# Two-block transformer forward on one Trainium2 core: convolution taps held in program sequence, and unsplit float32 products of attention weights and values in block 2

## The chip, the core and the metric

The kernel runs on one core of one Trainium2 chip. The core has a matrix engine (TensorE, PE in the profile, its weight loads PEld), a vector engine (VectorE, DVE), an activation engine (ScalarE, ACT), a general engine (GpSimd, POOL) and a queue that issues transfers (SyncE, SP). The metric is device time of one execution in microseconds, the median of several. TensorE runs at one of two levels of its clock, 1.2 or 2.4 GHz; the profile gives the granted share (0.50 or 1.00).

## What is computed

Two different transformer blocks of two layers each, on 256 tokens of width 1024, in float32.

Block 1 has a second stream of 256 context tokens. Each of its layers runs a token mixer with three branches, a gated merge of them, and a SwiGLU feed-forward. The first layer runs both streams (512 columns), the second only the first one (256). Two pieces of the mixer matter here:

```python
def conformer_conv(h, w_glu, conv_w, conv_b, ln_g, ln_b, w_proj):
    u = h @ w_glu
    u = u[..., :CONV_CH] * jax.nn.sigmoid(u[..., CONV_CH:])
    u = depthwise_conv(u, conv_w, conv_b)        # width 31, 512 channels
    u = layer_norm(u, ln_g, ln_b)
    return jax.nn.silu(u) @ w_proj

def diff_attend(q, k, v, lam):                   # 8 heads, two halves of 64 each
    s = jnp.einsum('bhiqd,bhikd->bhiqk', q, k).astype(jnp.float32) * (HEAD_DIM ** -0.5)
    p = jax.nn.softmax(s, axis=-1)
    a = (p[:, :, 0] - lam * p[:, :, 1]).astype(v.dtype)
    return jnp.einsum('bhqk,bhkd->bhqd', a, v)
```

Block 2 has a layer with causal attention under a top-k mask (12 heads), a layer with three dilated groups (4 heads each, one softmax over the three), and in both an attention over 256 memory tokens (4 heads). Heads are 64 wide. Each is a softmax over scores and then the product of its weights p with the values v, `einsum('bhsm,bmhd->bshd', p, v)`. A feed-forward follows in each layer, and one norm at the end.

## The kernel before

Activations lie transposed, channels on the 128 partitions and tokens along the free axis. Nearly all products are made in three passes: each operand is split in a rounded part (hi, in the type fp32r that TensorE takes in one pass) and the rest (lo), and `mm3` (lines 160 to 166) issues hi by hi, hi by lo and lo by hi into one PSUM tile. Weights come by DMA as `raw` tiles of 1 MB. ACT writes their hi (`whi`, line 154) and DVE, for a few of them POOL, subtracts it from raw (`wlo`, line 155). PSUM has eight banks: six tiles `p` for linear layers and scores, two tiles `tr` for transposes, sums and products with values.

The program is a list of steps. `merge` interleaves side steps with the main ones in proportion to a cost. `emit` runs the steps in that order and so records the instructions. A scheduler then orders them on each engine by its own model of time and readiness, which may put an instruction far ahead of where it was recorded. `pin` (line 454) takes one instruction out of that freedom: it stays in the sequence of the program. Before the change only memsets and some transfers are pinned.

**The convolution** (`conv_tap`, lines 783 to 798). For channel tiles m = 0 and 1 a tap is one DVE instruction, acc = u * w + acc (line 796; the first one, with the bias, line 790). For m = 2 and 3 ACT multiplies (line 793) and POOL adds (line 794). There are 31 taps for each tile and layer. The first 20 steps go beside the projections of head pair 0, the rest in four equal parts beside the four rounds of `qkv(pr+1)` and `att(pr)`: the projections of the next pair of heads and the attention of this one.

**The round around it.** `qkv` makes q and k tiles in PSUM, and DVE and ACT take them out: a shuffle (718), two multiplies and an add of the rotary embedding (719, 720, 726), the split (257 and 258), and the split of the context half (260 and 261). The last of them, line 261 for k or for a scaled q, releases the `p` tile. `att_s` makes scores (`scores2`, line 743: two halves of 64 partitions, one instruction each in turn), DVE takes the maximum (853), ACT the exponential (856), DVE the reciprocal, a factor and the difference (860, 862, 863). `att_t` transposes the result (PE, 871), ACT copies it out (873), and `att_v` multiplies it with the values in unsplit float32 (881).

**Block 2's products with values.** `val_split` (1239) splits the values, `at_split` (1265) transposes a tile of softmax weights (PE, 1270) and splits it with ACT and DVE (257 and 258), and `values` (1250) makes for each of two heads three passes with 128 columns of values, of which only the head's own 64 rows of the result are used. Head 0 goes to columns 0 to 255 of a `tr` tile and head 1 to columns 256 to 511. Two ACT (1261) and two DVE instructions (1263) on 64 partitions each write the split output `O`, which the output projection multiplies. There are 12 calls of `values`: six in the top-k layer, two in the dilated one, and two for the memory in each.

Of the kernel before, what the change touches and what calls it, by code (L numbers as in the profile page):

```python
# [7 lines left out]
F32R = mybir.dt.float32r  # L8
I32 = mybir.dt.int32
AF = mybir.ActivationFunctionType  # L10
ALU = mybir.AluOpType
# [19 lines left out]
class Piece:  # L31
    hi = lo = prep = at = None
# [13 lines left out]
class Kern:  # L46
# [701 lines left out]
    def mixer1(self, l, hs, N, evac_y, mid):  # L748

        nc, a = self.nc, self.a  # L750
# [3 lines left out]
        V = {}  # L754
        P = lambda name: self.par[name, l]
# [27 lines left out]
        def conv_tap(m, k):  # L783
            if k == 0:
                V["ca", m] = self.slot()
            acc = V["ca", m][:, :N].rearrange("p (s t) -> p s t", s=nseg)
            u = V["u", m][:, :nseg, k + 1:k + 257]
            w = self.convw[l][:, 4 * k + m:4 * k + m + 1]
            if k == 0:
                nc.vector.tensor_scalar(acc, u, w, P("conv_b")[:, m:m + 1], op0=ALU.mult, op1=ALU.add)  # L790
            elif m >= 2:
                t = self.slot()[:, :N].rearrange("p (s t) -> p s t", s=nseg)
                nc.scalar.activation(t, u, AF.Copy, scale=w)  # L793
                nc.gpsimd.tensor_tensor(acc, acc, t, op=ALU.add)  # L794
            else:
                nc.vector.scalar_tensor_tensor(acc, u, w, acc, op0=ALU.mult, op1=ALU.add)  # L796
            if k == 30:
                V.pop(("u", m))

# [238 lines left out]
        out = []  # L1038
# [197 lines left out]
            nc.scalar.activation(p, p, AF.Copy, scale=r)  # L1236
        return p

    def val_split(self, ps, nh, sc=None):

        n = 64 * nh
        if n <= 256:
            t = self.slot(F32R)
            out = [t[:, :n], t[:, 256:256 + n]]
        else:
            out = [self.slot(F32R)[:, :n] for _ in range(2)]
        self.split(out[0], out[1], ps[:, :n], sc)
        return out

    def values(self, O, terms):  # L1250


        nc = self.nc
        ps = self.tr_ps()
        for h in range(2):
            for j, (v, p, c) in enumerate(terms[h]):
                self.mm3(ps[:, 256 * h + c:256 * h + 256], v, p, j == 0, j == len(terms[h]) - 1)
        hi, lo = O
        rows = [(slice(64 * h, 64 * h + 64), ps[64 * h:64 * h + 64, 256 * h:256 * h + 256]) for h in range(2)]
        for r, x in rows:  # L1260
            nc.scalar.activation(hi[r], x, AF.Copy)
        for r, x in rows:
            nc.vector.tensor_tensor(lo[r], x, hi[r], op=ALU.subtract)

    def at_split(self, p, nk, key, t, V):

        nc = self.nc
        ps = self.tr_ps()
        for k in range(nk):
            nc.tensor.transpose(ps[:, 128 * k:128 * k + 128], p[:, 128 * k:128 * k + 128], self.ident)  # L1270
        hi, lo = V[key]
        self.split(hi[:, t, :nk], lo[:, t, :nk], ps[:, :128 * nk].rearrange("p (k q) -> p k q", q=128))

    def mem_kv(self, l):

        nc, a, V = self.nc, self.a, self.v
        st = []
        Wm = a[f"l{l}_w_mem_kv_2"]

        def k_evac(m, ps):  # L1280
            if m == 0:
                V["mk", l] = self.acts(2, 256)
            self.split(*V["mk", l][m], ps[:, :256])

        self.lin(st, Wm, 0, 256, lambda: V["mh", l], 256, k_evac)

        def v_evac(t, ps):
            V["mv", l, t] = self.val_split(ps, 4)
# [87 lines left out]
    def mem_att(self, l, base, O):  # L1376

        nc, V = self.nc, self.v
        st = []

        def s_(h, t):
            if h % 2 == 0:
                V["ms"] = [self.s_ps()[:, :256] for _ in range(2)]
                self.scores2(V["qm", h // 2], V["mk", l][h // 2], slice(128 * t, 128 * t + 128), slice(0, 256), V["ms"])
            s = V["ms"][h % 2]
            V["mp", h, t] = self.softmax(s[:, :256], 256, V["rc"][:, t:t + 1])

        def n_(h, t):
            V["mp", h, t] = self.norm(*V["mp", h, t])

        def t_(h, t):
            if t == 0:
                V["mat", h] = [self.slot(F32R).rearrange("p (t k q) -> p t k q", t=2, k=2) for _ in range(2)]
            self.at_split(V.pop(("mp", h, t)), 2, ("mat", h), t, V)

        def v_(g):
            self.values(O()[base + g], [[([v[:, 128 * g:128 * g + 128] for v in V["mv", l, k]],
                                          [p[:, :, k] for p in V["mat", 2 * g + h]], 0)
                                         for k in range(2)] for h in range(2)])

        return self.pipe([(2 * g + h, t) for g in range(2) for t in range(2) for h in range(2)], s_, n_, t_, v_)
# [47 lines left out]
    def dsa(self, l):  # L1449
        nc, a, V = self.nc, self.a, self.v  # L1450
# [95 lines left out]
            V["qm", m] = p  # L1546

        def v_evac(t, ps):
            V["v", t] = self.val_split(ps, 4, V["rc"][:, t:t + 1])
# [29 lines left out]

        def t_(m, half, t):  # L1580
            if t == 0:
                V["aat", m, half] = [self.slot(F32R).rearrange("p (t k q) -> p t k q", t=2, k=2) for _ in range(2)]
            self.at_split(V.pop(("ap", m, half, t)), t + 1, ("aat", m, half), t, V)
# [12 lines left out]
    def dilated(self, l):  # L1596
# [18 lines left out]

        def v_evac(g):
            def f(t, ps):
                V["v", g, t] = self.val_split(ps, 4, V["rc"][:, t:t + 1])
            return f

        def qm_evac(m, ps):
# [61 lines left out]
        def t_(h, t):  # L1683
            if t == 0:
                for g in range(3):
                    V["aat", h, g] = [self.slot(F32R).rearrange("p (t k q) -> p t k q", t=2, k=2) for _ in range(2)]
            p = V.pop(("ap", h, t))
            for g in range(3):
                self.at_split(p[g // 2][:, 256 * (g % 2):], t + 1, ("aat", h, g), t, V)

        def v_(m):
            self.values(V["O"][m], [[([v[:, 128 * m:128 * m + 128] for v in V["v", g, k]],
                                      [p[:, k:, k] for p in V["aat", 2 * m + h, g]], 128 * k)
                                     for k in range(2) for g in range(3)] for h in range(2)])

        att = self.pipe([(2 * m + h, t) for m in range(2) for t in range(2) for h in range(2)], s_, n_, t_, v_)
# [228 lines left out]
```

## Time and profile before

| | |
|---|---|
| median of 3 runs | 2344.86 us (2341.8 to 2348.15) |
| the profiled execution, its own time | 2343.53 us |
| its span, first to last instruction | 2341.8 us |
| mean granted TensorE clock | 0.966 |
| PE busy | 2188.9 us, 93% of the span |
| DVE busy | 1642.7 us, 70% |
| ACT busy | 1090.0 us, 47% |
| POOL busy | 536.1 us, 23% |

The profiled execution took 1.7 us more than its span, and stands 1.3 us under the median. PE is busy nearly all the time, so what counts is where it is not, and where its clock is at the lower level. Line 796, the taps on DVE, holds 2% of the chain that ended last.

### The profile page before, as it was taken

Reading aid. Unit: us, or ns where it says so; the run is one execution under the profiler, and the core shown is the slowest. Engines: PE = TensorE matmul, PEld = TensorE weight load, DVE = VectorE, ACT = ScalarE, POOL = GpSimd, SP = SyncE. Lnnn points to the kernel's source line nnn. Section 1 sums busy time; section 2 is a strip of 40 time slices with the busy share of each in tenths; the row PEclk is TensorE's granted clock in tenths of the full one; section 3 lists DMA queues with packets and bytes.
Section 4 is the critical chain, followed back from the end, with each engine's and each line's share of the span. In section 5 each row is a group of like instructions: output and inputs, shape, how many; then the busy total and the mean of one; then the engine's idle time right before and its main releaser. Section 6 shows DMA issues by size and latency. Waiting matters only on the chain.

```text
span 2341.8 us, 37618 instructions
## 1 busy us (share of the span) xinstructions
PE 2188.9 (93%) x14576; PEld 1990.2 (85%) x14576; DVE 1642.7 (70%) x3315; ACT 1090.0 (47%) x2110; POOL 536.1 (23%) x545
## 2 busy tenths in 40 slices
PE   4978899999989999998999999899989999999998
PEld 3767777788888888888898999899967999998998
DVE  5585865958778855567977877765686765687665
ACT  5335565333332222233566655554456554565543
POOL 2344343221340111042333312100353000210000
PEclk9989999999999999997999999999988999999999
DMA  7311121345514555553322454465441555542553
GB/s 272 93 55 56 53 73 56 105 151 168 174 37 155 166 180 175 162 165 127 126 73 81 149 171 163 144 203 178 153 110 39 166 186 178 187 145 91 181 184 123
DMA packets 296627, 319.20 MB, mean 136 GB/s; under 512 B 20544, under 2 KB 264352, under 8 KB 296448
## 3 DMA queue, kind: packets, MB, share of 16 engines
q1 hardware_dynamic: 293072, 311.27, 41.3%
q0 software_dynamic: 2224, 3.43, 0.6%
q8 instruction: 114, 1.87, 0.3%
q10 hardware_dynamic: 1152, 2.10, 0.3%
q14 instruction: 65, 0.53, 0.1%
HBM read 315.72 MB, written 1.05 MB: 135 GB/s over the span
## 4 chain that ended last, share of the span: by engine, by line
PE 69%; DVE 18%; ACT 4%; issue 4%; DMA 2%; POOL 2%; ACTq 0%; DVEq 0%; POOLq 0%; SPq 0%
PE p L164 20%; PE p L165 19%; PE p L166 19%; DVE wlo L155 3%; DVE t L796 2%; DVE t L478 2%; PE p L743 2%; PE p L247 1%; PE p L249 1%; PE p L248 1%; PE tr L881 1%; ACT whi L154 1%; DMA mraw<-in_w_mod_dram 1%; DVE b L853 1%; PE tr L484 1%
## 5 line engine op out<-in xcount | busy, mean ns | idle before, releaser
L164 PE MATMUL p<-t,whi 128*128 128x256 f32 (+1 forms) x3724 | 1176.5, 320 | 18.3 <-ACT t L560 7.1
L166 PE MATMUL p<-t,wlo 128*128 128x256 f32 (+1 forms) x3724 | 1178.1, 318 | 10.4 <-DVE wlo L155 5.9
L165 PE MATMUL p<-t,whi 128*128 128x256 f32 (+1 forms) x3724 | 1181.5, 318 | 5.5 <-DVE t L261 1.7
L164 PEld LDWEIGHTS p<-t,whi 128*128 128x128 f32 x3724 | 716.8, 194 | 69.7 <-ACT t L560 8.3
L166 PEld LDWEIGHTS p<-t,wlo 128*128 128x128 f32 x3724 | 721.3, 194 | 55.6 <-DVE wlo L155 7.6
L165 PEld LDWEIGHTS p<-t,whi 128*128 128x128 f32 x3724 | 722.1, 194 | 50.2 <-DVE t L659 3.5
L154 ACT ACTIVATE whi<-raw 128x1024 fp32r<-128x1024 f32 (+4 forms) x487 | 491.5, 1020 | 536.0 <-PE p L165 335.1
L155 DVE TENSOR_TENSOR wlo<-raw,whi 128x1024 fp32r<-128x1024 f32 (+4 forms) x443 | 547.7, 1238 | 204.9 <-ACT whi L154 107.5
L155 POOL TENSOR_TENSOR wlo<-raw,whi 128x1024 fp32r<-128x1024 f32 (+2 forms) x44 | 103.9, 2362 | 525.7 <-ACT whi L154 507.0
L478 DVE SCALAR_TENSOR_TENSOR t<-mraw,big,t 128x512 f32<-128x512 f32 x224 | 173.2, 811 | 16.9 <-DMA mraw<-in_w_mod_dram 15.2
L794 POOL TENSOR_TENSOR t<-t,t 128x512 f32<-128x512 f32 (+1 forms) x120 | 131.8, 1098 | 181.0 <-ACT t L793 171.3
L299 POOL TENSOR_TENSOR t<-t,t 128x256 f32<-128x256 f32 (+1 forms) x27 | 25.3, 935 | 426.1 <-ACT t L297 375.8
L260 ACT ACTIVATE t<-t 128x256 fp32r<-128x256 f32 (+1 forms) x115 | 54.3, 473 | 146.5 <-DVE t L689 110.9
L594 POOL TENSOR_TENSOR t<-t,t 128x256 f32<-128x256 f32 (+1 forms) x68 | 69.6, 1053 | 225.3 <-ACT t L596 224.6
L743 PE MATMUL p<-t,t 64*128 64x256 f32 (+2 forms) x528 | 80.9, 380 | 30.1 <-DVE t L261 18.8
L247 PE MATMUL p<-whi,t 128*128 128x256 f32 x352 | 102.7, 292 | 0.8 <-ACT t L856 0.8
L249 PE MATMUL p<-whi,t 128*128 128x256 f32 x352 | 100.4, 285 | 0.0
L248 PE MATMUL p<-wlo,t 128*128 128x256 f32 x352 | 100.0, 284 | 0.0
L257 ACT ACTIVATE t<-p 128x256 fp32r<-128x256 f32 x76 | 29.1, 383 | 149.1 <-DVE p L726 118.3
L796 DVE SCALAR_TENSOR_TENSOR t<-u,big,t 128x512 f32<-128x512 f32 (+1 forms) x120 | 97.2, 810 | 1.8
L689 DVE TENSOR_TENSOR t<-t,p 128x256 f32<-128x256 f32 (+1 forms) x91 | 43.1, 474 | 75.6 <-PE p L166 75.5
L743 PEld LDWEIGHTS p<-t,t 64*128 64x128 f32 x528 | 52.6, 212 | 51.1 <-issue 26.3
(303 smaller groups left out, 2633.9 us busy)
## 6 DMA issues: line engine op xcount, KB each, us to landing
raw<-in_w_in_dram SPq DMA_DIRECT2D x60, 1024.0 KB, 5.1
raw<-in_l_w_gate_up_dram SPq DMA_DIRECT2D x44, 1024.0 KB, 5.1
raw<-in_w_ffn_in_dram SPq DMA_DIRECT2D x42, 1024.0 KB, 5.2
mraw<-in_w_mod_dram SPq DMA_DIRECT2D x80, 512.0 KB, 4.1
raw<-in_l_w_in_dram SPq DMA_DIRECT2D x15, 1024.0 KB, 5.1
raw<-in_l_w_down_dram SPq DMA_DIRECT2D x16, 896.0 KB, 4.9
t<-in_w_mod_dram SPq DMA_DIRECT2D x32, 256.0 KB, 5.4
raw<-in_w_attn_out_dram SPq DMA_DIRECT2D x8, 1024.0 KB, 5.3
```

The source lines that it names most:

```text
L154: nc.scalar.activation(p.hi, src, AF.Copy)
L155: eng.tensor_tensor(p.lo, src, p.hi, op=ALU.subtract)
L164: mm(ps, lh, rh, start=first, stop=False)
L165: mm(ps, lh, rl, start=False, stop=False)
L166: mm(ps, ll, rh, start=False, stop=last)
L247: mm(ps[:, :256], lh, p.hi[:, k % 4], start=k == 0, stop=False)
L248: mm(ps[:, :256], lh, p.lo[:, k % 4], start=False, stop=False)
L249: mm(ps[:, :256], ll, p.hi[:, k % 4], start=False, stop=k == 7)
L478: nc.vector.scalar_tensor_tensor(acc, w[:, k], c, acc, op0=ALU.mult, op1=ALU.add)
L743: self.nc.tensor.matmul(out[half], q[i // 2][h, qs], k[i % 2][h, ks], start=i == 0, stop=i == 2)
L794: nc.gpsimd.tensor_tensor(acc, acc, t, op=ALU.add)
L796: nc.vector.scalar_tensor_tensor(acc, u, w, acc, op0=ALU.mult, op1=ALU.add)
```

## The change

Two things. Every tap's DVE or ACT instruction is pinned (POOL's adds are not). And in block 2 neither the values nor the transposed softmax weights are split: each product with values is one float32 matmul with the head's own 64 columns, head 0 on the column half of the array that gives partitions 0 to 63 and head 1 on the other, in turn, into the same 256 columns of one `tr` tile. The output is split in one piece, by one ACT and one DVE instruction on 128 partitions.

```diff
             if k == 0:
-                nc.vector.tensor_scalar(acc, u, w, P("conv_b")[:, m:m + 1], op0=ALU.mult, op1=ALU.add)
+                i = nc.vector.tensor_scalar(acc, u, w, P("conv_b")[:, m:m + 1], op0=ALU.mult, op1=ALU.add)
             elif m >= 2:
                 t = self.slot()[:, :N].rearrange("p (s t) -> p s t", s=nseg)
-                nc.scalar.activation(t, u, AF.Copy, scale=w)
+                i = nc.scalar.activation(t, u, AF.Copy, scale=w)
                 nc.gpsimd.tensor_tensor(acc, acc, t, op=ALU.add)
             else:
-                nc.vector.scalar_tensor_tensor(acc, u, w, acc, op0=ALU.mult, op1=ALU.add)
+                i = nc.vector.scalar_tensor_tensor(acc, u, w, acc, op0=ALU.mult, op1=ALU.add)
+
+            self.pin(i)
...
-        for h in range(2):
-            for j, (v, p, c) in enumerate(terms[h]):
-                self.mm3(ps[:, 256 * h + c:256 * h + 256], v, p, j == 0, j == len(terms[h]) - 1)
-        hi, lo = O
-        rows = [(slice(64 * h, 64 * h + 64), ps[64 * h:64 * h + 64, 256 * h:256 * h + 256]) for h in range(2)]
-        for r, x in rows:
-            nc.scalar.activation(hi[r], x, AF.Copy)
-        for r, x in rows:
-            nc.vector.tensor_tensor(lo[r], x, hi[r], op=ALU.subtract)
+        n = len(terms[0])
+        for j in range(n):
+            for h in range(2):
+                v, p, c = terms[h][j]
+                nc.tensor.matmul(ps[64 * h:64 * h + 64, c:256], v, p, start=j == 0, stop=j == n - 1)
+        self.split(*O, ps[:, :256])
 
-    def at_split(self, p, nk, key, t, V):
+    def at_copy(self, p, nk, key, t, V):
...
-        hi, lo = V[key]
-        self.split(hi[:, t, :nk], lo[:, t, :nk], ps[:, :128 * nk].rearrange("p (k q) -> p k q", q=128))
+        nc.scalar.activation(V[key][:, t, :nk], ps[:, :128 * nk].rearrange("p (k q) -> p k q", q=128), AF.Copy)
...
-            self.values(V["O"][m], [[([v[:, 64 * kv:64 * kv + 128] for v in V["v", k]], [p[:, k:, k] for p in x[h]],
+            self.values(V["O"][m], [[(V["v", k][:, 64 * (kv + h):64 * (kv + h) + 64], x[h][:, k:, k],
                                       128 * k) for k in range(2)] for h in range(2)])
```

`val_copy` stands in the place of `val_split` in the same way: one ACT instruction, with the token's scale where there is one. The calls for the memory and the dilated layer change as the last one shown does.

How the instructions move on DVE in block 1's first layer, between the projections of head pair 1 and its last release of a `p` tile (line 261). `t_980<-u_766` is a tap, `wlo` a weight's lo part. Before:

```order
L796 SCALAR_TENSOR_TENSOR t_980<-u_766,big,t_980 128x512
L258 TENSOR_TENSOR t_1112<-p_1086,t_1111 128x256
L796 SCALAR_TENSOR_TENSOR t_980<-u_766,big,t_980 128x512 x9
L155 TENSOR_TENSOR wlo_1254<-raw,whi_1253 128x1024
L796 SCALAR_TENSOR_TENSOR t_980<-u_766,big,t_980 128x512
L155 TENSOR_TENSOR wlo_1258<-raw,whi_1257 128x1024
L796 SCALAR_TENSOR_TENSOR t_980<-u_766,big,t_980 128x512 x4
L718 STREAM_SHUFFLE t_1288<-p_1261 128x256
L719 TENSOR_TENSOR p_1261<-p_1261,t_610 128x256
L155 TENSOR_TENSOR wlo_1365<-raw,whi_1364 128x1024
L726 TENSOR_TENSOR p_1261<-p_1261,t_1288 128x256
```

After:

```order
L258 TENSOR_TENSOR t_1112<-p_1086,t_1111 128x256 x2
L796 SCALAR_TENSOR_TENSOR t_980<-u_766,big,t_980 128x512 x5
L155 TENSOR_TENSOR wlo_1254<-raw,whi_1253 128x1024
L155 TENSOR_TENSOR wlo_1258<-raw,whi_1257 128x1024
L718 STREAM_SHUFFLE t_1288<-p_1261 128x256
L719 TENSOR_TENSOR p_1261<-p_1261,t_610 128x256
L155 TENSOR_TENSOR wlo_1365<-raw,whi_1364 128x1024
L726 TENSOR_TENSOR p_1261<-p_1261,t_1288 128x256
L855 TENSOR_REDUCE b_1302<-p_1303 128x1
L258 TENSOR_TENSOR t_1287<-p_1261,t_1286 128x256
L855 TENSOR_REDUCE b_1302<-p_1304 128x1
L261 SCALAR_TENSOR_TENSOR t_1287<-p_1261,t_1286 128x256
```

From the start of the taps to this line 261 there are 26 taps of line 796 before, and 9 after. Before, the 60 taps of the layer stand in two runs of 30. After, those taken out of the runs stand further on, in ones and twos, between the instructions of all the rounds.

On PE, one call of `values` in the top-k layer. The tile written is its PSUM tile, the first one read holds the transposed softmax weights of one head, and the second one values. Before:

```order
L164 MATMUL tr_17633<-t_17395,t_16793 128x256
L165 MATMUL tr_17633<-t_17396,t_16793 128x256
L166 MATMUL tr_17633<-t_17395,t_16793 128x256
L164 MATMUL tr_17633<-t_17395,t_16837 128x128
L165 MATMUL tr_17633<-t_17396,t_16837 128x128
L166 MATMUL tr_17633<-t_17395,t_16837 128x128
L164 MATMUL tr_17633<-t_17407,t_16793 128x256
L165 MATMUL tr_17633<-t_17408,t_16793 128x256
L166 MATMUL tr_17633<-t_17407,t_16793 128x256
L164 MATMUL tr_17633<-t_17407,t_16837 128x128
L165 MATMUL tr_17633<-t_17408,t_16837 128x128
L166 MATMUL tr_17633<-t_17407,t_16837 128x128
```

After:

```order
L1267 MATMUL tr_17623<-big,t_17549 128x128 x2
L1259 MATMUL tr_17602<-t_17385,t_16789 64x256
L1259 MATMUL tr_17602<-t_17395,t_16789 64x256
L1259 MATMUL tr_17602<-t_17385,t_16832 64x128
L1259 MATMUL tr_17602<-t_17395,t_16832 64x128
```

Twelve matmuls of 128 output rows became four of 64, heads in turn.

## Rows read from the trace of the kernel before

**Rows 1.** The page: granted clock in 40 slices, in tenths

```profile
PEclk9989999999999999997999999999988999999999
```

**Rows 2.** Stretches: length, busy us (count) per engine, clock, DMA share, GB/s

```profile
core 0: us, PE busy (x) PEld busy (x) DVE busy (x) ACT busy (x) POOL busy (x), PEclk, DMA share, GB/s
110.00:172.00 62.00, 48.26 (x258) 41.25 (x257) 55.98 (x83) 22.77 (x47) 25.45 (x18) 0.89 0.21 68
172.00:250.00 78.00, 71.67 (x430) 59.84 (x429) 44.73 (x112) 46.79 (x119) 35.53 (x28) 0.96 0.17 55
250.00:312.00 62.00, 51.21 (x292) 42.66 (x290) 57.33 (x105) 32.66 (x85) 23.09 (x17) 0.92 0.16 52
312.00:400.00 88.00, 85.12 (x497) 70.03 (x496) 42.21 (x99) 53.80 (x130) 33.16 (x26) 1.00 0.22 73
```

**Rows 3.** Timeline of PE: start, us, instruction, count [idle before <-its end]

```profile
163.16 0.98 PE L743 MATMUL p<-t,t 64*128 64x256 f32 x3 [13.74 <-DVE t L261]
...
222.35 0.48 PE L164 MATMUL p<-t,whi 128*128 128x512 f32 x1 [2.80 <-DVE t L261]
...
281.01 0.98 PE L743 MATMUL p<-t,t 64*128 64x256 f32 x3 [5.04 <-DVE t L261]
```

**Rows 4.** Waits of PE by layer: us, times, longest

```profile
PE tr L871 <- DVE t L863: 6.9, 6, 2.5
...
PE tr L871 <- DVE t L863: 6.1, 2, 3.2
```

**Rows 5.** Timeline of DVE, taps of the first layer

```profile
141.19 11.42 DVE L796 SCALAR_TENSOR_TENSOR t<-u,big,t 128x512 f32<-128x512 f32 x9
...
153.66 0.74 DVE L796 SCALAR_TENSOR_TENSOR t<-u,big,t 128x512 f32<-128x512 f32 x1
```

**Rows 6.** Stretches, line 796 alone: DVE busy (count), clock, DMA

```profile
117.40:163.16 45.76, 29.25 (x26) 0.91 0.21 69
...
1165.50:1168.76 3.26, 1.91 (x3) 0.92 0.41 121
```

**Rows 7.** Stretches behind two of the waits, columns as in group 2

```profile
163.16:168.10 4.94, 4.94 (x13) 3.85 (x14) 4.83 (x12) 3.10 (x10) 1.77 (x2) 0.50 0.00 0
281.01:287.50 6.49, 6.49 (x17) 5.00 (x18) 4.83 (x12) 3.10 (x10) 1.70 (x2) 0.50 0.00 0
```

**Rows 8.** Timeline of PE, a call of `values` in either layer

```profile
1801.41 0.28 PE L164 MATMUL tr<-t,t 128*128 128x256 f32 x1
...
1802.74 0.41 PE L1270 MATMUL tr<-big,t 128*128 128x128 f32 x2
...
2118.84 0.39 PE L164 MATMUL tr<-t,t 128*128 128x256 f32 x1 [0.49 <-DVE t L258]
...
2123.03 0.41 PE L1270 MATMUL tr<-big,t 128*128 128x128 f32 x2
```

**Rows 9.** Timeline of PE: unsplit products (line 881), row halves (line 743)

```profile
172.43 1.06 PE L881 MATMUL tr<-t,t 128*128 128x128 f32 x8
173.42 0.38 PE L743 MATMUL p<-t,t 64*128 64x256 f32 x2
...
1740.81 0.28 PE L165 MATMUL p<-t,whi 128*128 128x256 f32 x1
1740.93 0.28 PE L166 MATMUL p<-t,wlo 128*128 128x256 f32 x1
1741.13 0.62 PE L743 MATMUL p<-t,t 64*128 64x256 f32 x6
```

**Rows 10.** Waits of PE, top-k attention, then dilated attention

```profile
PE tr L1270 <- DVE t L258: 2.8, 1, 2.8
...
PE p L164 <- ACT t L1261: 1.1, 2, 0.6
...
PE tr L1270 <- DVE t L258: 2.0, 4, 0.7
...
PE p L164 <- ACT t L1261: 1.5, 2, 0.9
```

More of the change, by code (lines that the diff above doesn't have):

```diff
@@ L1237, in norm, with val_copy @@
         return p
[L1239 to L1244, printed above, removed]
-        else:
-            out = [self.slot(F32R)[:, :n] for _ in range(2)]
-        self.split(out[0], out[1], ps[:, :n], sc)
-        return out
+    def val_copy(self, ps, nh, sc=None):
+        t = self.slot()[:, :64 * nh]
+        if sc is None:
+            self.nc.scalar.activation(t, ps[:, :64 * nh], AF.Copy)
+        else:
+            self.nc.scalar.activation(t, ps[:, :64 * nh], AF.Copy, scale=sc)
+        return t
     def values(self, O, terms):
@@ L1287, in v_evac @@
         def v_evac(t, ps):
-            V["mv", l, t] = self.val_split(ps, 4)
+            V["mv", l, t] = self.val_copy(ps, 4)
         self.lin_nat(st, Wm, 256, lambda t: [(h[:, 128 * t:128 * t + 128], lo[:, 128 * t:128 * t + 128])
@@ L1392, in t_ @@
             if t == 0:
-                V["mat", h] = [self.slot(F32R).rearrange("p (t k q) -> p t k q", t=2, k=2) for _ in range(2)]
-            self.at_split(V.pop(("mp", h, t)), 2, ("mat", h), t, V)
+                V["mat", h] = self.slot().rearrange("p (t k q) -> p t k q", t=2, k=2)
+            self.at_copy(V.pop(("mp", h, t)), 2, ("mat", h), t, V)
         def v_(g):
-            self.values(O()[base + g], [[([v[:, 128 * g:128 * g + 128] for v in V["mv", l, k]],
-                                          [p[:, :, k] for p in V["mat", 2 * g + h]], 0)
+            self.values(O()[base + g], [[(V["mv", l, k][:, 128 * g + 64 * h:128 * g + 64 * h + 64], V["mat", 2 * g + h][:, :, k], 0)
                                          for k in range(2)] for h in range(2)])
@@ L1548, in v_evac @@
         def v_evac(t, ps):
-            V["v", t] = self.val_split(ps, 4, V["rc"][:, t:t + 1])
+            V["v", t] = self.val_copy(ps, 4, V["rc"][:, t:t + 1])
         self.lin(rest, W, 1864, 256, hs, 256, qm_evac)
@@ L1581, in t_ @@
             if t == 0:
-                V["aat", m, half] = [self.slot(F32R).rearrange("p (t k q) -> p t k q", t=2, k=2) for _ in range(2)]
-            self.at_split(V.pop(("ap", m, half, t)), t + 1, ("aat", m, half), t, V)
+                V["aat", m, half] = self.slot().rearrange("p (t k q) -> p t k q", t=2, k=2)
+            self.at_copy(V.pop(("ap", m, half, t)), t + 1, ("aat", m, half), t, V)
         def v_(m):
@@ L1617, in f @@
             def f(t, ps):
-                V["v", g, t] = self.val_split(ps, 4, V["rc"][:, t:t + 1])
+                V["v", g, t] = self.val_copy(ps, 4, V["rc"][:, t:t + 1])
             return f
@@ L1685, in t_ @@
                 for g in range(3):
-                    V["aat", h, g] = [self.slot(F32R).rearrange("p (t k q) -> p t k q", t=2, k=2) for _ in range(2)]
+                    V["aat", h, g] = self.slot().rearrange("p (t k q) -> p t k q", t=2, k=2)
             p = V.pop(("ap", h, t))
             for g in range(3):
-                self.at_split(p[g // 2][:, 256 * (g % 2):], t + 1, ("aat", h, g), t, V)
+                self.at_copy(p[g // 2][:, 256 * (g % 2):], t + 1, ("aat", h, g), t, V)
         def v_(m):
-            self.values(V["O"][m], [[([v[:, 128 * m:128 * m + 128] for v in V["v", g, k]],
-                                      [p[:, k:, k] for p in V["aat", 2 * m + h, g]], 128 * k)
+            self.values(V["O"][m], [[(V["v", g, k][:, 128 * m + 64 * h:128 * m + 64 * h + 64], V["aat", 2 * m + h, g][:, k:, k], 128 * k)
                                      for k in range(2) for g in range(3)] for h in range(2)])
```

## The prediction

> **What bounds the kernel now.** I read the page first. PE is busy 93% of the span, so time can be won only where PE stands idle, works at the lower level of its clock, or does work that goes away. The page's row of the granted clock is full nearly everywhere; its slices are 58.5 us wide and hide short stretches at 0.50 [rows 1]. So I cut the stretch of the first layer's taps in four: the two in which line 796 runs in bulk (110 to 172 and 250 to 312), and the two without taps on DVE [rows 2]. The reader is to see there how DVE and PE go together. In the stretches with taps DVE is busy 55.98 and 57.33 of 62 us and PE lacks 13.7 and 10.8 us; in those without, DVE has 33 and 46 us to spare and PE lacks 6.3 and 2.9.
>
> The timeline of PE then names the three long waits [rows 3]. All end with line 261 on DVE, the release of a `p` tile at the end of a round's projections: 13.74, 2.80 and 5.04 us. The middle one is the same wait in a round without any tap ahead of it. So 2.80 is what this place costs by itself, and the rest of the other two is DVE's backlog. The timeline of DVE shows the backlog: nine taps in a row, 11.42 us, and later ones of 0.74 us [rows 5]. From the first tap to PE's restart at 163.16, 26 taps hold DVE for 29.25 of 45.76 us [rows 6].
>
> **The change, part by part**, against the profiled execution (span 2341.8, its own time 2343.53 us, which lies 1.3 us under the median of 2344.86).
>
> *Taps, first layer.* No instruction is added or removed; the 60 taps of DVE move. Ahead of the first long wait 9 taps stand instead of 26, as the order of DVE shows. The 17 that go were worth at least 17 x 0.74 = 12.6 us [rows 5] and at their mean of 29.25 / 26 = 1.12 us [rows 6] 19 us, which is more than the 10.9 us by which the wait exceeds 2.80. So I let it fall to 2.80: **-10.9**. The third wait falls likewise from 5.04: **-2.2**. PE restarts after both at the lower level: 4.94 and 6.49 us of uninterrupted work at 0.50 [rows 7], which at 1.00 would take half. I count all of the first gain and half of the second, since a wait of 2.80 us stays: -2.5 - 1.6 = **-4.1**. (With no gain in clock this term is 0; with all of it, -5.7.)
>
> Against this, taps now stand between the maximum, the factor and the difference of each attention step, and PE's transposes wait for the difference (line 871 for line 863: 6.9 us in 6 waits [rows 4], of 32 steps in this layer). The trace shows no round with taps in ones and twos. Bounds: nothing new, where every tap falls in DVE's idle time, or one tap in every step, 32 x 0.74 = 24 us, and 41 at the 1.27 us of the run of nine. I take a value near the lower bound, because DVE has 33 and 46 us to spare in the rounds that get the taps, 15 taps each: a tap in one of five steps, +5 us, less 3 us of the old 6.9 which fall in the third stretch, where the taps become fewer: **+2**.
>
> ACT's taps, pinned too, and POOL's adds behind them keep their number. ACT is busy 46.79 of 78 us in the fullest of these stretches, and POOL 35.53 [rows 2]; their idle time covers it. Without that cover ACT's split of the weights would be late, and PE with it. The queue of transfers keeps its order and moves 52 to 73 GB/s here [rows 2]: nothing.
>
> *Taps, second layer.* Two waits for line 863 make 6.1 us [rows 4], and in the 3.26 us ahead of one of them three taps hold DVE for 1.91 [rows 6]. Half of 6.1 goes, and 1.5 comes back in other steps: **-1.5** (from -6.1 to +8, the second being 16 steps with a tap of about 0.5).
>
> *Products with values, on PE.* A call before: in the top-k layer 1802.74 - 1801.41 = 1.33 us for 12 matmuls; in the dilated one 2123.03 - 2118.84 = 4.19 us for 36 [rows 8]; for the memory 12 matmuls of 256 columns at a step of 0.12 us [rows 9], 1.44. Six, two and four calls: 8.0 + 8.4 + 5.8 = 22.1 us. After: an unsplit product with 128 moving columns is two records, and four of them take 173.42 - 172.43 = 0.99 us with a change of tiling at the end [rows 9]. A change of tiling costs 0.20 instead of 0.12 us (1740.93 to 1741.13 [rows 9]), so 0.91 / 4 = 0.23 us each, and 0.46 with 256 columns. One after the other: 6 x 1.38 + 4 x 1.84 + 2 x 4.14 = 23.9 us, and the change of tiling, twice in each of 12 calls, 1.9: 25.8 in all, +3.7. In pairs, the two column halves at once: 13.9, or -8.2. The nearest row for pairs is that of the two row halves: six of 256 columns take 0.62 us [rows 9], where a step of 0.12 and a last one of 0.28 would make 0.88. So halves do run together. As each product is two records and heads alternate only by product, I add half a product a call, 12 x 0.2: **-6** (bounds -8.2 and +3.7).
>
> The Trainium skill speaks against this part. "TensorE: Matmul & The Clock Gate", Part 3, "The mechanism", says that a weight load overlaps a running matmul only if its row group differs, and column halves share their rows. By that rule the halves would not overlap so freely, and the sum would hold +3.7 in the place of -6. The trace does not bear it out for whole-array matmuls, whose weight loads lie beside other matmuls (59.84 us of loads and 71.67 of matmuls in 78 [rows 2]). No row here shows column halves. It is a rival below.
>
> *Copies around them.* `at_copy` drops 64 subtractions on DVE, and `values` halves 24 ACT and 24 DVE instructions; the 12 subtractions of the values go too. Most lie beside PE's work: nothing. On the path: PE waits four times for the subtraction to release a `tr` tile in the dilated layer, 2.0 us, which goes; the same wait of 2.8 in the top-k layer I leave, as ACT ends late there. PE waits four times for line 1261, 1.1 + 1.5 us [rows 10]; one ACT instruction instead of two takes some 0.4 off each: **-3.5** together (bounds 0 and -7.4, all four rows).
>
> Sum: -10.9 - 2.2 - 4.1 + 2 - 1.5 - 6 - 3.5 = -26.2. From 2343.5 that is 2317.3, and with the 1.3 us to the median 2318.6: **2319 us**. If the column halves were in series it would be 2328.
>
> **The rivals.**
>
> 1. *Column halves in series.* PE's order has the heads in turn, but two records of one head stand next to each other, and pairs are shown for row halves alone. Price +3.7 for -6: **2328**. Chance 0.20.
>
> 2. *DVE gives part of it back.* A tap beside a POOL add costs more (1.27 in the run of nine against 0.74 [rows 5]), and the taps go to stretches in which POOL is busy 35.53 of 78 us [rows 2]. With one tap exposed in every second step, 16 x 0.74 = 12 in the first layer for 5, and 4 for 1.5 in the second: +9.5, **2328**. Chance 0.15.
>
> 3. *The long wait is not the taps.* It could be that the `p` tile would come late anyway, since a shuffle, a weight's subtraction, maxima and splits stand ahead of its release too. Then only block 2 gains: 9.5 us or, with halves in series, nothing, **2335 to 2345**. Against it speaks the same place at 2.80 us without taps [rows 3]. Chance 0.10.
>
> 4. *Slower: the chain of each attention step takes the taps.* The 32 steps of the first layer and 16 of the second run maximum, exponential, factor, difference, transpose one behind the other. If one tap were exposed in each, it would be 32 x 1.27 = 41 for 5 and 16 x 0.6 = 10 for 1.5, +44: **2363**. It decides from 0.7 us a step on, where the new waits (33 us) eat the gain and what I had counted for them. Against it: PE has projections between a step's scores and its transposes, so that line 871 waited for line 863 8 times in 48 steps. Chance 0.05.
>
> **How the numbers follow.** The forecast holds 0.50. A measurement of this kernel tells 0.3% from no change, 7 us. Faster by more (under 2337.8): the forecast, rivals 1 and 2, and half of rival 3 would make 0.90; I take 0.05 off for rivals 1 and 2 coming together with a late restart: 0.85. Within 0.3%: 0.10. Slower: 0.05. The range goes down to 2304, where nothing new waits, line 871's 6.9 us go and the halves pair fully (about -2 - 5 - 4 - 4 against the forecast), and up to 2337, rivals 1 and 2 together.
>
> **What would show it.** Right: PE's wait at the end of round 1 under 4 us; line 796 spread over all four stretches, with DVE between 48 and 60 us in each; PE's granted clock in 110 to 172 above 0.95; a top-k call of `values` near 0.9 us; no wait of line 1270's successor for a subtraction. Wrong: PE's idle time before line 871 above 15 us in the first layer (rivals 2 and 4); a call of 1.4 us or more (rival 1); a wait above 8 us still at line 261 (rival 3).

## The result, and the profile after

The changed kernel takes 2311.3 us, the median of 4 runs (2308.62 to 2312.47); the kernel before took 2345.55 beside it (4 runs, 2341.8 to 2348.15). The ratio is 0.9847 with a 95% interval of 0.9833 to 0.9861: faster by 34 us where 26 were forecast (2319, range 2304 to 2337). The profiled span went from 2341.8 to 2308.5 us.

To see where the 33.3 us of span came from, I cut both traces at the same instructions of PE: from the last transpose of line 322 to line 316 behind the first layer's attention, from there to the second layer's attention (which ends at the transposes of line 1319, later 1315), then to block 2's top-k layer, and at both ends of its two attention parts. Each column of times is one execution, the profiled one.

| stretch | before, us | after, us | difference |
|---|---|---|---|
| first layer with its taps | 315.2 | 298.7 | -16.5 |
| from there to the second layer's attention | 726.9 | 729.3 | +2.4 |
| second layer's attention and taps | 213.4 | 212.7 | -0.7 |
| up to block 2's top-k layer | 337.0 | 336.2 | -0.8 |
| top-k attention with its memory | 147.8 | 140.4 | -7.4 |
| between | 198.7 | 198.2 | -0.5 |
| dilated attention with its memory | 111.7 | 102.4 | -9.3 |
| the rest, both ends | 291.1 | 290.7 | -0.4 |

Busy times in three of these stretches, from the view by stretches (columns as in [rows 2]), first of before, then of after:

```profile
97.10:412.30 315.20, 279.92 (x1569) 232.97 (x1569) 214.82 (x438) 163.82 (x386) 121.72 (x96) 0.95 0.19 64
...
1689.60:1837.40 147.80, 127.87 (x881) 112.90 (x880) 110.73 (x364) 84.07 (x233) 57.08 (x69) 0.87 0.32 86
...
2036.10:2147.80 111.70, 104.49 (x815) 97.46 (x815) 88.66 (x276) 66.13 (x174) 19.71 (x23) 0.94 0.33 111
```

```profile
95.90:394.60 298.70, 275.27 (x1569) 228.72 (x1569) 221.32 (x434) 165.35 (x386) 124.44 (x96) 0.97 0.20 65
...
1672.80:1813.10 140.30, 124.17 (x846) 106.89 (x847) 95.85 (x322) 78.96 (x226) 57.85 (x69) 0.84 0.33 91
...
2011.30:2113.70 102.40, 97.61 (x776) 89.23 (x776) 74.93 (x234) 64.43 (x170) 19.57 (x25) 0.93 0.38 123
```

The first layer has the same 1569 matmuls. They hold PE for 4.65 us less, since more of them ran at the upper level of the clock, and PE stands idle for 11.85 us less. In the dilated part PE's busy time falls by 6.9 us with 39 fewer matmul records, and its idle time from 7.2 to 4.8.

The same four stretches of the first layer as in [rows 2], of after:

```profile
110.00:161.00 51.00, 46.62 (x252) 39.95 (x251) 40.45 (x66) 23.16 (x45) 24.74 (x18) 0.93 0.25 83
161.00:239.00 78.00, 71.22 (x423) 58.60 (x421) 57.91 (x125) 46.55 (x116) 35.60 (x28) 0.96 0.17 55
239.00:294.00 55.00, 50.13 (x314) 42.56 (x312) 41.86 (x87) 33.70 (x86) 23.48 (x17) 0.97 0.19 58
294.00:382.00 88.00, 82.29 (x478) 67.45 (x477) 64.95 (x116) 53.23 (x127) 34.90 (x25) 1.00 0.23 73
```

These windows only come near those of before. Cut at the very instructions of PE at which [rows 2] cuts, the two stretches that held the taps become some 9 to 10 us shorter each (52.5 and 52.6 for 62), the second 0.8 us longer and the fourth some 3 us longer (91.1 for 88). In the windows shown, line 796 has 12, 17, 12 and 20 instructions in them, where it had 30, 1, 30 and none. PE's long waits, in its timeline of after, answer to [rows 3]:

```profile
152.60 0.98 PE L743 MATMUL p<-t,t 64*128 64x256 f32 x3 [4.38 <-DVE t L261]
...
209.12 0.98 PE L743 MATMUL p<-t,t 64*128 64x256 f32 x3 [2.83 <-DVE t L261]
...
266.05 0.82 PE L743 MATMUL p<-t,t 64*128 64x256 f32 x3 [2.81 <-DVE t L261]
```

13.74, 2.80 and 5.04 us became 4.38, 2.83 and 2.81. Behind the first and the third PE still restarts at the lower level, and stays there for nearly the whole of the first stretch and half of the third (0.55 and 0.74 for 0.50 and 0.50 in [rows 7]):

```profile
152.60:157.54 4.94, 4.94 (x14) 3.88 (x15) 4.86 (x11) 3.52 (x10) 2.83 (x2) 0.55 0.00 0
...
266.05:272.54 6.49, 6.49 (x24) 5.19 (x25) 6.45 (x13) 4.09 (x12) 2.82 (x2) 0.74 0.00 0
```

How long PE now waits in front of the transposes, by layer (first layer, then second; [rows 4] had 6.9 and 6.1):

```profile
PE tr L873 <- DVE t L865: 4.2, 5, 1.7
...
PE tr L873 <- DVE t L865: 8.4, 4, 2.7
```

In the first layer PE also waits more for ACT, 5.5 us in all, where before it waited 0.8 us for line 856. First the row of before, then those of after:

```profile
PE p L247 <- ACT t L856: 0.8, 1, 0.8
```

```profile
PE p L247 <- ACT t L858: 2.7, 2, 1.6
...
PE p L743 <- ACT t L875: 1.5, 2, 1.1
PE p L743 <- ACT t L891: 1.3, 1, 1.3
```

And calls of `values`, top-k, memory and dilated, in PE's timeline of after ([rows 8]); a call runs from its first matmul to the start of what follows:

```profile
1782.74 0.87 PE L1259 MATMUL tr<-t,t 128*64 128x256 f32 x8
1783.55 0.44 PE L1267 MATMUL tr<-big,t 128*128 128x128 f32 x2
...
2047.80 1.08 PE L1259 MATMUL tr<-t,t 128*64 128x256 f32 x8
2048.81 0.39 PE L164 MATMUL p<-t,whi 128*128 128x256 f32 x1
...
2091.57 2.17 PE L1259 MATMUL tr<-t,t 128*64 128x256 f32 x24
2093.67 0.44 PE L1267 MATMUL tr<-big,t 128*128 128x128 f32 x2
```

1.33 became 0.81, 1.44 became 1.01, and 4.19 became 2.10 us. Not every call runs so: the first of the top-k layer takes 1.48 us at a clock of 0.50, and the two for the memory there take 1.21 and 1.84, the second with a product of line 743 among its records. All twelve as they ran take 14.6 us, where those of before took 24.0. PE waits no more for a subtraction there: of [rows 10], 2.0 us in the dilated part are now 0.9 for ACT's copy, and the waits for line 1261 are gone.

### The profile page after: what moved, and what is told of

The parts are those of the page before. It is cut to its first block, busy times and chain, and to the rows that moved or that the text cites. A ratio compares the mean times of both kernels' runs of the same rounds, so it can differ in the third digit from the quotient of the medians.

```text
span 2308.5 us, 37343 instructions
## 1 busy us (share of the span) xinstructions
PE 2175.2 (94%) x14512; PEld 1974.4 (86%) x14512; DVE 1622.4 (70%) x3227; ACT 1085.5 (47%) x2098; POOL 535.8 (23%) x545
## 4 chain that ended last, share of the span: by engine, by line
PE 73%; DVE 15%; ACT 4%; issue 3%; POOL 2%; DMA 1%; ACTq 0%; DVEq 0%; POOLq 0%
PE p L164 21%; PE p L165 21%; PE p L166 20%; DVE wlo L155 3%; PE p L743 1%; DVE t L478 1%; DVE t L796 1%; PE tr L883 1%; PE p L247 1%; PE p L249 1%; PE p L248 1%; PE tr L484 1%; DVE b L855 1%; PE tr L1267 1%; POOL t L794 1%
## 5 line engine op out<-in xcount | busy, mean ns | idle before, releaser
L796 DVE SCALAR_TENSOR_TENSOR t<-u,big,t 128x512 f32<-128x512 f32 (+1 forms) x120 | 102.2, 851 | 0.8
```

Source lines behind the costliest of these rows:

```text
L796: i = nc.vector.scalar_tensor_tensor(acc, u, w, acc, op0=ALU.mult, op1=ALU.add)
```

## Experiments

My theory after the result: the two parts add, the taps giving what the first layer shows and block 2 what its attention shows. Times are medians; "before" stands for the runs of the kernel before on the same chip.

**Each part alone.** The first kernel has the pins and the old block 2. The second has the new block 2 and no pins; its edit against the changed kernel is shown:

```diff
-            self.pin(i)
```

> Only the taps are pinned; block 2 is as before. Theory (the two parts add, the taps are worth what the first layer shows between the traces, about 16 us): span 2326, between 2322 and 2329; the wait at line 261 at the end of round 1 falls from 13.7 to 4 to 5 us, and block 2 takes as long as before (147.8 us for the top-k part, 111.7 for the dilated part). Rival 1 (the long wait shrinks only because block 2's change moved buffers or the order elsewhere): wait above 8 us, span 2336 to 2342. Rival 2 (the taps carry more than their layer shows, since block 2 starts from other conditions): span under 2320.

Measured: 2342.84 us (10 runs), before 2344.46, ratio 0.9986 (0.9975 to 0.9997). The wait fell to 4.59 us and the first layer from 315.2 to 301.9, as expected:

```profile
152.34 0.97 PE L743 MATMUL p<-t,t 64*128 64x256 f32 x3 [4.59 <-DVE t L261]
```

Yet the kernel is hardly faster, and its span of 2340.7 us lies where rival 1 had it, for another reason. From the first layer's end to block 2's top-k layer it needs 1288.3 us where before needed 1277.3. The mean granted clock doesn't tell the two apart: over all their runs it goes from 0.962 to 0.968 here and from 0.962 to 0.966 before. Block 2's attention is not shorter, 461.0 us for 458.1 (here and below from the start of the top-k part to the end of the dilated one, with what lies between).

> Only block 2 is changed; the taps are free again. Theory (the parts add; block 2 is worth the 17 us by which its two attention parts became shorter between the traces): span 2325, between 2321 and 2328, with the first long wait back at 13 to 14 us. Rival (block 2 is worth only the 9.5 us of the prediction and the rest came with the taps): span 2331 to 2334, and the two attention parts of block 2 together shorter by about 10 us, not 17.

Measured: 2323.31 us, ratio 0.9920 (0.9903 to 0.9936). The first long wait is back at 13.70:

```profile
161.91 0.98 PE L743 MATMUL p<-t,t 64*128 64x256 f32 x3 [13.70 <-DVE t L261]
```

Block 2's attention takes 441.3 us, as in the changed kernel (440.9). So block 2 alone is worth 21 us, taps alone 1.6, and both 34: the parts don't add in these kernels. The theory holds for the stretches, and fails for the sum.

**Column halves in series.** The loops of `values` exchanged:

```diff
-        for j in range(n):
-            for h in range(2):
+        for h in range(2):
+            for j in range(n):
```

> The changed kernel with the loops of values exchanged: all products of the first head, then all of the second, on the same column halves; nothing else differs. Theory (the two column halves work at the same time when neighbours in the order use different halves): a dilated call goes from 2.1 to about 4.1 us, a top-k call from 0.8 to about 1.5, and the kernel is slower than the changed one by 8 to 12 us: span 2317 to 2321. Rival (the halves are in series anyway, or PE waits there for other engines, so that order does not matter): calls unchanged, span 2307 to 2311.

Measured: 2313.74 us, ratio 0.9869 (0.9854 to 0.9883). In its timeline of PE a top-k call and a dilated one:

```profile
1783.04 0.88 PE L1259 MATMUL tr<-t,t 128*64 128x256 f32 x8
1783.85 0.44 PE L1267 MATMUL tr<-big,t 128*128 128x128 f32 x2
...
2098.33 3.73 PE L1259 MATMUL tr<-t,t 128*64 128x256 f32 x24
2101.99 0.39 PE L166 MATMUL p<-t,wlo 128*128 128x256 f32 x1
```

The dilated call goes from 2.10 to 3.66 us: the halves do work at once, and there it takes alternation. The call with two products for each head keeps its 0.81 us, though both products of head 0 stand ahead of those of head 1. Its records start in the order of 256, 256, 256, 256, 128, 128, 128 and 128 columns, though the program has two of 256 and two of 128 of head 0 first. So PE itself brings work of the other half forward, at least two products (four records) far. With six products a head this comes too late for most of them: head 1 starts 1.57 us into the call, beside the last four of head 0's twelve records. Ten of twelve calls are of the short kind, so only the two dilated ones become longer, 3.1 us together, and the dilated part takes 104.8 us for 102.4. Both theories missed that.

The whole differs by 2.4 us, but other stretches move by more than that. Ahead of the first changed call this kernel has the changed kernel's instructions, in the same order and with the same places of its tiles, and yet the second layer's attention took 4.5 us longer (first the changed kernel, then this one):

```profile
1123.90:1336.60 212.70, 196.61 (x1462) 180.35 (x1460) 174.12 (x385) 129.04 (x288) 71.43 (x95) 1.00 0.31 101
```

```profile
1123.29:1340.53 217.24, 199.57 (x1462) 183.33 (x1460) 174.10 (x385) 129.03 (x288) 71.52 (x95) 0.98 0.30 99
```

So two executions of the same instructions can differ by 4 to 5 us in one stretch, and smaller differences between stretches of two traces show nothing by themselves.

**The copies put back.** Subtractions into a tile that nobody reads (for the transposed weights as shown, and for the values likewise), and four instructions instead of two behind `values`:

```diff
+        nc.vector.tensor_tensor(lo[:, t, :nk], x, V[key][:, t, :nk], op=ALU.subtract)
...
-        self.split(*O, ps[:, :256])
+        for r, x in rows:
+            nc.scalar.activation(hi[r], x, AF.Copy)
+        for r, x in rows:
+            nc.vector.tensor_tensor(lo[r], x, hi[r], op=ALU.subtract)
```

> The changed kernel with the dropped work of DVE and ACT put back: each transposed weight and each value gets its subtraction again, into a tile that nobody reads, and values writes its result in two ACT and two DVE instructions instead of one and one; the products stay unsplit on column halves. Theory (of the 17 us of block 2 some 8 are waits of PE for these copies, the rest the products): span 2316, between 2313 and 2319. Rival (the copies lie beside PE's work and the products carry it all): 2307 to 2311. Forecast of the prediction for this part: 3.5 us, 2312.

Measured: 2334.22 us (2328.71 to 2336.89), ratio 0.9955 (0.9939 to 0.9971), 23 us above the changed kernel, where 5 to 10 were expected. Block 2's attention takes 449.9 us for 440.9, so by these two traces the copies are worth 9.0 there (8 were expected). The other kernels with the new block 2 and without the copies have 436.8 to 444.1, so 6 to 13 is as much as can be said. In the dilated part PE waits for subtractions again:

```profile
PE tr L1277 <- DVE t L1281: 2.0, 4, 0.7
...
PE p L164 <- ACT t L1268: 1.1, 2, 0.9
```

But 16 us more were lost between the first layer and block 2's top-k layer (1294.3 us for 1278.1, in the slowest of this kernel's four runs, 2336.89 us). There this kernel has the changed kernel's instructions, in the same order on each engine but for a handful, and four of its own subtractions late in the stretch, 0.41 us each. 10.0 of the 16 us are lost before the second layer's attention ends, ahead of all of these. An edit in block 2 can reach there only through where tiles lie: the pool's slots are handed out for the whole program, and hundreds of instructions ahead of block 2 wait for another release than before.

**The same order, other places.** 64 unused columns more in the tile of constants move tiles to other places and change no order on any engine:

```diff
-CONSTS = 1536
+CONSTS = 1600
```

> The changed kernel with 64 more columns reserved in the tile of constants, which nobody uses: every instruction stands in the same order on its engine, but tiles get other places in SBUF, and several hundred instructions wait for other releases. Theory P (the places set waits all over the kernel, and with them PE's clock; that is what the single edits lost or won outside their own stretches): own stretches as in the changed kernel (283 us in the first layer, 441 in the attention of block 2), the middle stretch off by up to 15 us from its 1280, and the time off from 2311 by more than 3 us. Rival N (places don't matter; the middle stretch follows from the change itself): 2308 to 2314.

> Taps alone, with the same 64 unused columns. Theory P: the first layer's 287 us stay, the middle stretch is not again the 1290 of the first such kernel but anywhere between 1276 and 1296; time 2328 to 2348, by more than 3 us off from 2342.8. Rival N: 2340 to 2346 with a middle stretch of 1290 again, because the taps' gain is paid back there.

> Block 2 alone, with the same 64 unused columns. Theory P: the attention of block 2 stays at 441 us, the middle stretch moves from 1277; time 2320 to 2340. Rival N: 2320 to 2326.

> The kernel before with the same 64 unused columns and no other edit. Theory P: first layer 300 and block 2's attention 458 us as before, the middle stretch off from 1280, time off from 2344.5 by more than 3 us. Rival N: ratio 1.000 within 0.0015. If theory P holds, the mean over both placements of taps alone against before is the better price of the taps: 10 to 13 us by their own stretch.

These expectations cut the first layer some 15 us shorter and the middle some 2 us longer than my table does.

| kernel | time, us | same with 64 columns | first layer | middle | block 2's attention |
|---|---|---|---|---|---|
| before | 2344.46 | 2345.93, ratio 0.9995 (0.9980 to 1.0009) | 315.2, 312.8 | 1277.3, 1280.9 | 458.1, 460.1 |
| taps alone | 2342.84 | 2329.62, 0.9927 (0.9912 to 0.9943) | 301.9, 297.7 | 1288.3, 1283.0 | 461.0, 460.9 |
| block 2 alone | 2323.31 | 2319.84, 0.9887 (0.9868 to 0.9905) | 313.4, 311.4 | 1273.5, 1273.4 | 441.3, 439.6 |
| both | 2311.3 | 2310.49, 0.9840 (0.9820 to 0.9860) | 298.7, 297.6 | 1278.1, 1280.2 | 440.9, 439.3 |

"Middle" runs from the first layer's end to block 2's top-k layer. Three of the four kernels move by 0.8 to 3.5 us, as rival N had it or within 0.2 us of it. Taps alone moves by 13, as theory P had it; its runs with the old places (2337.38 to 2344.56) and with the new (2328.13 to 2331.06) don't overlap. So places are not always worth much, but they can be worth as much as the taps, and that one kernel's 1.6 us was its places. The totals don't add in the new places either: 16 us for the taps, 26 for block 2 and 35 for both.

The stretches of their own hold in both places. All nine kernels of this study with DVE's taps pinned in the first layer take 297.4 to 301.9 us there, and all four without these pins 311.4 to 315.2; in the four pairs that differ by the taps alone the gain is 13.3 to 15.1. Block 2's attention gains 17 to 22 by its edit and nothing by the taps. From trace to trace these stretches move by up to 4 us too.

One wait shows how it happens. In both kernels with taps alone the same instruction of ACT, a scaled copy into a new slot (line 580), first with the old places, then with the new:

```profile
1034.20 0.51 ACT L580 ACTIVATE t<-t,c 128x256 f32<-128x256 f32 x1 [4.60 <-POOL t L594]
```

```profile
1027.55 0.49 ACT L580 ACTIVATE t<-t,c 128x256 f32<-128x256 f32 x1
```

With the old places ACT stands 4.60 us for POOL's line 594, and what it makes next comes late. PE's next two waits in the timelines, old places and then new:

```profile
1041.06 0.58 PE L166 MATMUL p<-t,wlo 128*128 128x256 f32 x1 [3.56 <-DVE wlo L155]
1044.26 0.59 PE L611 MATMUL tr<-big,t 128*128 128x1 f32 x2 [2.40 <-DVE t L594]
```

```profile
1035.05 0.39 PE L166 MATMUL p<-t,wlo 128*128 128x256 f32 x1 [1.01 <-DVE wlo L155]
1040.20 0.59 PE L611 MATMUL tr<-big,t 128*128 128x1 f32 x2 [4.64 <-DVE t L594]
```

The two waits together are 5.96 and 5.65 us, so nearly nothing is lost directly. But the granted clock in the 38 us around them, from the same place of the program on, is 0.73 with the old places and 0.82 with the new:

```profile
1026.00:1064.00 38.00, 29.23 (x174) 28.35 (x174) 23.69 (x53) 12.14 (x23) 14.77 (x13) 0.73 0.41 132
```

```profile
1024.00:1062.00 38.00, 29.63 (x198) 28.85 (x198) 29.01 (x68) 13.60 (x25) 17.33 (x13) 0.82 0.41 133
```

PE gets through 24 matmuls more in the same time, and is 2.8 us further ahead at the end of it. What in these waits sets the clock, no run shows. This is one place. Of the 11.4 us between the two spans (2340.7 and 2329.3), 5.3 lie in the middle, 4.2 in the first layer and 1.7 ahead of it; that the rest is of the same kind, I did not follow wait by wait.

**Pins of the first layer only**, in both places:

```diff
-            self.pin(i)
+            if l == 0:
+                self.pin(i)
```

> The changed kernel with the taps pinned in the first layer alone; in the second layer they are free as before. Theory (the pins of the second layer give nothing: PE's waits for line 865 there came to 8.4 us after for 6.1 before): the same or faster by 1 to 3 us, 2308 to 2312, and the stretch from the second layer's attention to its end 210 to 213 us for 212.7. Rival (the second layer gained the 1.5 us of the prediction or more): 2312 to 2316. Where tiles get other places, 3 us more either way.

> The same with 64 unused columns in the tile of constants, so with other places of the tiles and the same order. Theory: within 4 us of the one without, own stretches equal to within 2 us. Rival (the pins of the second layer decide, not the places): equal within 1.5 us, both on the same side of the changed kernel.

Measured: 2312.37 us, ratio 0.9867 (0.9850 to 0.9883), and 2305.43, 0.9839 (0.9824 to 0.9853). The second layer's attention takes 211.4 and 210.8 us for 212.7 and 214.0 with pins, which is less than two executions of the same instructions can differ there. PE's waits for the difference tell more: 5.2 and 3.9 us for 8.4 and 7.0. They are 6.8 to 8.4 us in all six kernels with every tap of that layer pinned, and 3.9 to 6.1 in all six with none. So the pins of the second layer cost some 2 to 3 us of waits. The totals can't show it: the two differ by 7 us from places alone, where at most 4 were expected, and their first layers, 301.9 and 297.9 us, by 4.0, where at most 2 were expected.

**No taps on DVE.** The 120 instructions of line 796 are left out, so the convolution is incomplete:

```diff
-                i = nc.vector.scalar_tensor_tensor(acc, u, w, acc, op0=ALU.mult, op1=ALU.add)
+                i = None
...
```

> Leaves out the 120 taps of line 796 on DVE in both layers (those of the first two channel groups but for the first tap), so the convolution is incomplete; all else as in the changed kernel. It prices what the spread taps still cost. Theory (some of them stand in front of what PE waits for): PE's waits for lines 865 and 261 in the first layer, 14.2 us, fall by 5 to 9, those for line 865 in the second from 8.4 to under 4; time 2294 to 2303. Rival (spread, they lie in DVE's idle time): 2307 to 2313. The prediction's +2 net and 5 exposed corresponds to 2303 to 2306.

Measured: 2294.0 us (2292.0 to 2298.45). The first layer takes 288.5 us for 298.7, the second layer's attention 207.3 for 212.7. PE's waits in the first layer, and its busy time there:

```profile
PE p L164 <- DVE t L261: 8.7, 3, 2.9
PE tr L874 <- DVE t L866: 3.7, 4, 1.1
```

```profile
95.00:383.50 288.50, 269.50 (x1571) 224.12 (x1571) 159.82 (x376) 163.78 (x386) 119.55 (x96) 0.99 0.21 70
```

So the spread taps still cost some 10 and 5 us. In the first layer 4.4 of them are idle time of PE and 5.8 busy time, at a clock of 0.97 for 0.99; the two waits that I had named fall by only 1.8, to 12.4 us, so the 5 to 9 expected of them were wrong and the total right. Against 315.2, all of DVE's taps of the first layer cost 26.7 us in the order before, and the change took 16.5 of it. And without one of them, line 261 still makes PE wait 2.9 us at most in each of three rounds: that is the place's own cost.

**DVE's taps alone pinned**, ACT's and the first taps of channel tiles 2 and 3 free:

```diff
-            self.pin(i)
+            if m < 2:
+                self.pin(i)
```

> The changed kernel with only DVE's taps (and the first tap of every group that lies on DVE's side, groups 0 and 1) pinned; the taps on ACT and the first taps of groups 2 and 3 are free. Theory (DVE's order alone carries the gain of the first layer): first layer 297 to 300 us as in the changed kernel, time 2308 to 2315. Rival (ACT's order carries part of it, since POOL's adds and the splits follow it): first layer above 302 us, time above 2316.

Measured: 2303.26 us (2298.91 to 2306.13), ratio 0.9827 (0.9810 to 0.9844), the fastest complete kernel of the study. Its first layer takes 297.4 us, so ACT's pins carry nothing of the gain. That it is 8 us faster than the changed kernel I don't put down to them either: its own stretches account for 1.3 (first layer) and 1.9 (second), 4.1 lie in the top-k attention, which the edit doesn't touch, and places alone have moved a kernel by 7 and by 13. One row goes further. In the second layer PE's waits for the difference are here

```profile
PE tr L874 <- DVE t L866: 4.4, 3, 2.1
```

as in the kernels without any pins there. So the rise to 8.4 us seems to come with ACT's pinned taps and not with DVE's; with one kernel that is a hint and not shown.

## Why the prediction was right, and where it was off

- **Taps, first layer: -15.2 forecast, -16.5 measured** (13.3 to 15.1 in the four pairs of kernels that differ by the taps alone). The long wait fell to 4.38 us instead of 2.80, the third to 2.81 as forecast. That 2.80 is this place by itself is shown by the kernel without DVE's taps (2.9). So the 17 taps that went were not quite all of the backlog: nine still stand ahead of the release, and 1.5 us of wait with them. That the sum comes so near is partly luck, as the waits show: line 261 gave 11.6 us of 13.1, the waits for the reciprocal (2.6 us for line 860) and the difference fell by 5.3 where +2 was forecast, and those for ACT, put at nothing, rose by 4.7.
- **The clock: -4.1 forecast.** Not where I looked: PE still restarts at the lower level behind 4.38 us, and the first stretch came to 0.93, not above 0.95. But over the layer the same matmuls hold PE for 4.65 us less.
- **New waits behind taps: +2.** Line 865 costs PE 4.2 us for 6.9 in the first layer, so less than I allowed for, and only 0.5 more than without any tap on DVE. What the spread taps cost lies elsewhere: 5.8 of the 10 us against no taps on DVE are busy time of PE at a lower clock, and the waits for ACT are 5.5 us for 2.3. As a whole it is twice the 5 that I took for exposed taps. The premise of rival 2 holds: in the four stretches line 796 takes 65.7 us for 61.8 with the same taps. A tap takes 0.74 us where no add of POOL runs beside it (35 of the 60 taps before, 15 after).
- **Second layer: -1.5 forecast, -0.7 measured**, and against the kernels without pins there +1.3 and +3.2, all within what two executions differ by. The step "half of 6.1 goes, and 1.5 comes back" had the wrong sign: waits for line 865 rose from 6.1 to 8.4 us. That looks like rival 2, and rival 4 in small, but with DVE's taps alone pinned the waits are 4.4 us.
- **Products: -6 forecast, -9.0 measured.** Six calls at 0.81, four at 1.01 and two at 2.10 make 13.1 us, for 22.1; as they ran, 14.6 for 24.0, so -9.4. The price of a pair was right. The half product that I added to each call, "as each product is two records", was not there, and neither was the change of tiling twice a call: the last record of a dilated call is followed after 0.20 us where a record with 128 columns takes 0.10, 0.1 us once. Rival 1 falls by the calls, and by the run in series from the other side. The rule of the Trainium skill, "TensorE: Matmul & The Clock Gate", Part 3, "The mechanism", that I set against this part would, as I read it, have kept halves with the same rows apart; the trace does not agree (24 records in 2.10 us, and 3.66 in series). "TensorEngine Tiling (Array Packing)", section "Key Properties", says in the Trainium skill that different tiles can execute weight loads and matmuls in parallel; with that the trace agrees.
- **Copies: -3.5 forecast, about -8 measured** (17.2 in block 2's attention less 9.0 for products; 9.0 when put back, within 6 to 13). This is the step that was sized worst: I took only PE's waits with a row of their own, and "most lie beside PE's work: nothing" left out that DVE has 14.9 and 13.7 us less to do in the two parts and can be earlier with other work that PE waits for. Which of these waits made it up is not shown. -7.4 was my bound.
- **Places of tiles: not in the prediction.** It forecast by stretches, and in the changed kernel the middle stretch happened to stay (1278.1 for 1277.3). With other places the same reasoning would have met 2330 or 2343 for taps alone.
- **Rival 3** falls with the wait at 4.38 and with the first layer's gain in every pair.

Of the signs that I had named for being right, three came: the taps in all four stretches, a top-k call of 0.81 us, and no wait for a subtraction there. Three did not: the first wait is 4.38 us and not under 4, the clock of the first stretch 0.93 and not above 0.95, and DVE is busy 40 to 65 us in the four stretches and not 48 to 60. Of the signs for being wrong one came in name only: two calls took more than 1.4 us, one at the lower clock and one with another product among its records.

Range and sign held; the 8 us that were missing lie in block 2, products 3 and copies 4.5.

## What to carry to other kernels

Count what stands ahead of a release on its engine's queue: 26 filler instructions ahead of one made 13.7 us, nine left 4.4, and the price of the place with none (2.9) tells when to stop. Where two products with 64 columns of weights wait for the same engine, put them on the two column halves, and alternate where a head has many products; the copies that an unsplit product spares can be worth about as much as PE's own time (here some 8 or 9 us each). And in a kernel whose buffers are handed out by a program, change the places and nothing else once before pricing a part by a few us: here that alone moved one kernel by 13. Nor does one trace of each kernel price a stretch to a few us: the same instructions took 212.7 and 217.2 us in two executions.

## What I had not expected of the hardware

- The two column halves are filled without strict order: with the products of one head ahead of the other's, a call of two products a head took 0.81 us both ways, one of six 3.66 for 2.10.
- Nearly equal waits in the same place can go with a different clock: two pairs of 5.96 and 5.65 us went with 0.73 and 0.82 over 38 us, and with 2.8 us of time. What decided between them is not shown.
